# Layer 0's banded attention and the projection's first tiles, put in order by the kernel's list scheduler

## The chip, the cores and the metric

The kernel runs on one core of a Trainium2 chip. The core has a matrix engine (TensorE, PE in the profile; its weight loads are PEld), a vector engine (VectorE, DVE), a scalar engine (ScalarE, ACT), a general engine (GpSimd, POOL) and a queue engine that starts transfers (SyncE, SP). Each works through its own queue in order and waits on semaphores for the others. The metric is the device time of one execution in microseconds (us). TensorE's clock has two levels, 1.2 and 2.4 GHz; the profile gives it as a share of the upper one.

## The reference

Two transformer layers over 256 latent and 256 context tokens of width 1024, then a second block of another kind. All of it is fp32. Only layer 0's mixer matters here:

```
def even_mixer(u_ctx, u_lat, w_in, w_out, a_prm, sink, rope_ang, need_ctx):
    p_ctx = u_ctx @ w_in
    p_lat = u_lat @ w_in
    a_lat, a_ctx = rwkv7_mixer(p_ctx[..., :A_IN], p_lat[..., :A_IN], a_prm, need_ctx)
    qc, kc, vc = split_qkv(p_ctx[..., A_IN:], B_HEADS, B_KV_HEADS)
    ql, kl, vl = split_qkv(p_lat[..., A_IN:], B_HEADS, B_KV_HEADS)
    ql, kl = axial_rope(ql, rope_ang), axial_rope(kl, rope_ang)
    b_lat = banded_window_attention(ql, kl, vl, kc, vc, sink_g)
    b_ctx = context_attention(qc, kc, vc, sink_g)
    return concat(a_lat, b_lat) @ w_out, concat(a_ctx, b_ctx) @ w_out
```

One input projection feeds two things. Its attention part (8 query heads in two groups, 2 key and value heads, 64 wide) goes through a softmax that has a learned sink beside the scores. Its RWKV part is mixed with each token's neighbours (`centred_shift`) and then runs a recurrence in both directions. Layer 1 has two other kinds of attention; each layer ends with an MLP.

## The kernel before

**Products.** An fp32 operand is split into a high and a low part, and a product is three matmuls: high by high, high by low, low by high (`mmW`, lines 623 to 625). A weight chunk of 128x1024 comes by DMA into `raw`; ACT copies it to `whi` (line 608) and DVE subtracts to get `wlo` (line 609). In this part of the program the pool of `whi` and `wlo` has two buffers each.

**The stretch in question.** It has three pieces.

- Keys, values and four query tiles are projected over six PSUM tiles (`psT`). Each is evacuated by `evac_b`: an ACT copy into a ring of two buffers, rotary position (a matmul `psR`, line 944, and three DVE steps, lines 946 to 948) and the split into halves for the heads (`qB`, lines 962 and 963; `kBh` and `kBl`, lines 969 and 970).
- `b_attn` (line 1133) runs attention for 8 groups of four heads through `attn4`. For a head: scores in `psS` (two matmuls, line 1041, three PSUM banks in turn), the band's mask added by DVE (line 1048), the row maximum (line 1052), the sink (line 1057), the exponential on ACT with a sum (line 1059). For a pair of heads: the reciprocal and the normalisation of `P` on DVE and POOL (line 1068), the transposes `psP` (line 1077) and their copies to `PT`. Per group: eight output matmuls in `psO` (line 1087; one PSUM bank, written as halves of 64 columns of the array) and the split into `moBh` and `moBl` (lines 1090, 1091). The first four groups have 512 keys, the others 256.
- `proj_a` (lines 1134, 1135) computes 12 tiles of the RWKV part, each of 24 matmuls of 128x512 into `psT`, in two banks in turn. `evac_a` takes each out: an ACT copy with a scale (line 930) and two DVE steps for the neighbours (lines 931, 933). Tiles 12, 13 and 14 go to `lora`, the others to `rkv`.

Behind it the RWKV recurrence starts. Its first steps are kappa's square on DVE (`sq`), a sum over channels by matmul (`ssp`), a reciprocal root (`rsn`, on POOL) and its transposes (`psr`). Its pool (`rw`) lies where attention's buffers lay, so the square waits for the attention's last reader, a `psO` matmul.

**What sets the order.** There are two ways. Outside a marked stretch, the framework's own scheduler orders the instructions. Between `flow.open()` and `flow.close()` the kernel records every operation and orders it itself (class `_Flow`): `take` gives each operation an assumed duration, `links` its dependencies, including those by buffers in turn, and `order` issues, from what is ready first on the engine that can start first, the one with the longest chain behind it. For PE an operation of the current array shape has a bonus of 2000 ns. Neighbouring matmuls on the same tile are joined to one operation when short. The clock of this list starts at zero at the stretch's start: it does not know what the engines are still doing from before. Two stretches are ordered this way: the RWKV recurrence (`flow.open(2)`) and layer 1's attention (`flow.open()`). Everything issued so has the helper's line 501 in the profile. `b_attn` and `proj_a` were not in one.

Of the kernel before, what the change touches and what calls it, by code (L numbers as in the profile page):

```python
# [266 lines left out]
class _Flow:  # L267
# [47 lines left out]
    def take(self, key, op, f, a, k):  # L315
        is_ap = lambda x: isinstance(x, (tile.Tile, _View)) or isinstance(x, bass.AP) and isinstance(x.tensor, tile.Tile)
        aps = [x for x in list(a) + list(k.values()) if is_ap(x)]
        outs = [x for x in (a[0], k.get("accum_out")) if x is not None and is_ap(x)]
        o = _Op()
        o.key, o.calls, o.res = key, [(f, a, k)], [o]  # L320
        o.w = [self.touched(x) for x in outs]
        o.r = [self.touched(x) for x in aps if not any(x is y for y in outs)]
        n = math.prod(aps[0].shape[1:])
        psum = any(t_[3] for t_ in o.w + o.r)
        o.tail = 70
        if key == "T":
            mv, st = (a[1], a[1]) if op == "transpose" else (a[2], a[1])
            n = math.prod(mv.shape[1:]) if op != "transpose" else a[2].shape[1]
            size = lambda x: 32 if x <= 32 else 64 if x <= 64 else 128
            rows, cols = size(st.shape[0]), size(st.shape[1])  # L330
            cyc = 1 if mv.dtype == F32R else 2 if op == "transpose" else 4
            o.len, o.recs = max(n * cyc, 60 * min(cyc, 2)) / 2.4, 2 if cyc == 4 else 1
            o.cells = [(r, c) for r in range(4) if o.r[0][1] >> r & 1 for c in range(4) if o.w[0][1] >> c & 1]
            if mv.dtype == F32R:
                o.len += 11
            o.mode, o.tail, o.dur, o.grid, o.issue = (rows, cols), 270, 0, {}, 0
            o.first = op != "transpose" and k["start"] and not k.get("skip_group_check")
            o.more = op != "transpose" and not (k["start"] and k["stop"]) and not k.get("skip_group_check")
            o.parts = [(o.cells, o.len, o.recs)]
        elif key == "V":  # L340
            n = max(math.prod(x.shape[1:]) for x in aps)
            ins = sum(math.prod(x.shape[1:]) > 16 for x in aps if not any(x is y for y in outs))
            o.dur = 150 + 2.8 * n if op.endswith("scan") else 150 + 1.03 * n if psum else 170 + (self.both if ins > 1 else 1.2 if self.both > 1.5 else .65) * n
        elif key == "S":
            o.dur = 190 + .82 * n
        elif key == "G":
            o.dur = 1650 if k.get("op") == OP.pow else 200 + (1.3 if op == "tensor_scalar" and self.both > 1.5 else 2.4 if self.both > 1.5 or op != "tensor_scalar" else 3.2) * n
        elif key == "X":
            o.dur, o.tail = 0, 0
        else:  # L350
            o.dur, o.tail = 2800, 2500
        p = self.ops[-1] if self.ops else None
        if not (key == "T" and p is not None and p.key == "T" and p.mode == o.mode and
                (p.w[0][0] == o.w[0][0] and (p.dur < 800 or o.mode != (128, 128)) or self.one and p.one)):
            p = o
            self.ops.append(o)
        else:
            p.calls += o.calls
            p.res += o.res
            p.w += o.w  # L360
            p.r += o.r
            if key == "T":
                p.parts += o.parts
                p.first, p.more = p.first or o.first, p.more or o.more
        if key == "T":

            at = max([p.issue] + [p.grid.get(c, 0) for c in o.cells])
            p.issue = at + 7 * o.recs
            for c in o.cells:
                p.grid[c] = at + o.len  # L370
            p.dur = max(p.dur, p.issue, at + o.len)
            p.one = self.one
        return o
# [8 lines left out]
    def links(self):  # L382

        ops, seen = self.ops, {}
        for i, o in enumerate(ops):
            o.pre, o.at = set(), 0
            mine = [(x, True) for x in o.w] + [(x, False) for x in o.r]
            for (nm, q, m, ps), wr in mine:
                if isinstance(nm, _Root):
                    nm.ops.add(i)  # L390
                for j, q2, m2, wr2 in seen.get(nm, ()):
                    if q & q2 and ((wr or wr2) and m & m2 or ps and ops[j].key != o.key):
                        o.pre.add(j)
                    elif ps and q & q2 and wr and wr2 and o.key == "T" and o.first and ops[j].more and j != i:
                        o.pre.add(j)
            for (nm, q, m, ps), wr in mine:
                l = seen.setdefault(nm, [])
                if wr:
                    l[:] = [e for e in l if e[0] == i or e[1] & ~q or e[2] & ~m]
                l.append((i, q, m, wr))  # L400
        for g, names, ring in self.gates:
            k = ops.index(g)
            g.pre.update(i for i in range(k) if any(x[0] in names for x in ops[i].w + ops[i].r))
            for r in self.roots:
                if r.ring is ring:
                    for i in r.ops:
                        ops[i].pre.add(k)
        last = {}
        for r in self.roots:
            if r.heir is not None:  # L410
                was = {j for j, *_ in ()} | {i for i, o in enumerate(ops) if i < min(r.ops) and any(
                    x[0] is r.heir or x[0] == r.heir for x in o.w + o.r)}
            elif r.place is not None:
                was = last.get((id(r.ring), r.place), ())
                last[id(r.ring), r.place] = r.ops
            else:
                continue
            for i in r.ops:
                ops[i].pre.update(was)
        for i in range(len(ops) - 1, -1, -1):  # L420
            o = ops[i]
            o.way = getattr(o, "way", 0) + o.dur
            for j in o.pre:
                p = ops[j]
                p.way = max(getattr(p, "way", 0), o.way + (p.tail if p.key != o.key else 0))
# [81 lines left out]
def body(ctx: ExitStack, tc: tile.TileContext, A, out, dbg=None):  # L507
    nc = tc.nc
# [312 lines left out]
    def cpool(*cms):  # L821
        for cm in cms:
            opened.remove(cm)
            cm.__exit__(None, None, None)
# [305 lines left out]
    for t_ in S0s:  # L1130
        G.memset(t_, 0.0)

    b_attn()
    proj_a = lambda js, bank=None: gemm_T(W_in, [(j * 128, 128, j) for j in js], uh, ul, evac_a, bank=bank)
    proj_a((12, 13, 14) + tuple(x * 4 + t for t in range(3) for x in range(3)))
    cpool(cm_at, cm_attB)


# [1050 lines left out]
```

## Time and profile before

| | |
|---|---|
| median of 3 runs | 1804.53 us (1802.65 to 1807.39) |
| profiled execution | 1798.13 us, span 1796.2 us, mean clock 0.976 |
| PE busy | 1715.3 us (95%) |
| DVE, ACT, POOL busy | 60%, 49%, 25% |
| chain that ended last, PE | 86% |

The shares are means over the whole program. What one stretch can gain or lose is read from that stretch: whether PE waits in it, at which clock it runs, and which engine ends the waits. A wait appears in the timeline as a bracket behind the instruction that waited, with the engine and operation that released it.

### The profile page before, as it was taken

What the parts mean: (1) busy time and instruction counts of PE and PEld (TensorE: products, weight loads), DVE (VectorE), ACT (ScalarE), POOL (GpSimd) and SP (SyncE); (2) the same over time, 40 slices, a digit from 0 to 9 for tenths busy, and PEclk for the clock granted to TensorE, in tenths of its full rate; (3) what the DMA queues carried; (4) which work ended last, traced back from release to release, by engine and by line L of the source; (5) the groups of instructions that cost most, each with busy time, mean ns of one, the idle gap of its engine ahead of it and who ended that gap; (6) DMA issues with size and microseconds to landing.
All of it is one profiled execution on the core that took longest, in us unless ns stands there. A gap on an engine that the chain in (4) does not pass through costs nothing.

```text
span 1796.2 us, 33992 instructions
## 1 busy us (share of the span) xinstructions
PE 1715.3 (95%) x13601; PEld 1440.3 (80%) x13601; DVE 1082.0 (60%) x1965; ACT 884.1 (49%) x1703; POOL 447.2 (25%) x512
## 2 busy tenths in 40 slices
PE   6999899999898999999998999899989999999998
PEld 4777677767577888888887887799978889989997
DVE  3577577766656334444464775655566686568776
ACT  4555245544345554443443655545555554446553
POOL 1120344542413343333332213311120211110000
PEclk9999899999899999999998999999999999999999
DMA  9322141222264454444423322465547436655553
GB/s 311 108 59 60 37 140 51 96 74 95 72 198 142 131 169 147 141 141 141 141 82 87 89 71 71 132 197 187 188 152 226 129 93 174 190 156 187 177 183 121
DMA packets 185407, 240.08 MB, mean 134 GB/s; under 512 B 8961, under 2 KB 127889, under 8 KB 185121
## 3 DMA queue, kind: packets, MB, share of 16 engines
q1 hardware_dynamic: 183056, 229.68, 41.1%
q0 software_dynamic: 1904, 7.70, 1.3%
q8 instruction: 107, 1.75, 0.4%
q10 hardware_dynamic: 288, 0.52, 0.1%
q14 instruction: 52, 0.42, 0.1%
HBM read 236.83 MB, written 1.05 MB: 132 GB/s over the span
## 4 chain that ended last, share of the span: by engine, by line
PE 86%; DVE 5%; DMA 3%; ACT 2%; POOL 2%; issue 2%; SPq 0%; POOLq 0%; DVEq 0%; ACTq 0%
PE psT L623 9%; PE psT L625 9%; PE psT L624 9%; PE psT L501 9%; PE pf L628 6%; PE pf L629 6%; PE pf L630 6%; PE px L501 3%; PE ssp L501 2%; PE psr L501 2%; PE psU L623 2%; PE psU L625 2%; PE psU L624 2%; PE pq L501 2%; PE yp L501 2%; PE psS L501 2%
## 5 line engine op out<-in xcount | busy, mean ns | idle before, releaser
L609 DVE TENSOR_TENSOR wlo<-raw,whi 128x1024 fp32r<-128x1024 f32 x291 | 358.4, 1239 | 245.7 <-ACT whi L608 242.6
L608 ACT ACTIVATE whi<-raw 128x1024 fp32r<-128x1024 f32 x291 | 306.4, 1056 | 235.2 <-PE psT L624 121.6
L623 PE MATMUL psT<-uh,whi 128*128 128x256 f32 (+1 forms) x1032 | 332.4, 327 | 2.8 <-ACT uh L909 1.2
L624 PE MATMUL psT<-ul,whi 128*128 128x256 f32 (+1 forms) x1032 | 330.7, 321 | 0.0
L625 PE MATMUL psT<-uh,wlo 128*128 128x256 f32 (+1 forms) x1032 | 328.4, 321 | 0.0
L623 PEld LDWEIGHTS psT<-uh,whi 128*128 128x128 f32 x1032 | 193.3, 189 | 21.6 <-ACT uh L909 1.7
L624 PEld LDWEIGHTS psT<-ul,whi 128*128 128x128 f32 x1032 | 193.4, 188 | 17.9 <-issue 1.1
L625 PEld LDWEIGHTS psT<-uh,wlo 128*128 128x128 f32 x1032 | 193.5, 188 | 16.1 <-issue 0.3
L630 PE MATMUL pf<-whi,hlo 128*128 128x512 f32 x472 | 182.4, 390 | 0.0
L629 PE MATMUL pf<-wlo,hh 128*128 128x512 f32 x472 | 182.3, 390 | 0.0
L628 PE MATMUL pf<-whi,hh 128*128 128x512 f32 x472 | 181.9, 392 | 0.0
L1512 POOL TENSOR_TENSOR ffr<-ffr 128x512 f32<-128x512 f32 (+1 forms) x64 | 64.3, 1004 | 283.2 <-ACT hh L1511 251.7
L630 PEld LDWEIGHTS pf<-whi,hlo 128*128 128x128 f32 x472 | 88.6, 188 | 18.8 <-issue 0.2
L629 PEld LDWEIGHTS pf<-wlo,hh 128*128 128x128 f32 x472 | 88.6, 188 | 17.5
L628 PEld LDWEIGHTS pf<-whi,hh 128*128 128x128 f32 x472 | 88.5, 188 | 17.5
L623 PE MATMUL psU<-uh,whi 128*128 128x256 f32 x352 | 99.0, 282 | 1.0 <-DVE cv L2101 1.0
L624 PE MATMUL psU<-ul,whi 128*128 128x256 f32 x352 | 98.5, 280 | 0.0
L625 PE MATMUL psU<-uh,wlo 128*128 128x256 f32 x352 | 98.5, 280 | 0.0
L1513 DVE TENSOR_TENSOR hlo<-ffr,hh 128x512 fp32r<-128x512 f32 (+1 forms) x64 | 47.6, 743 | 76.9 <-POOL ffr L1512 76.9
L717 POOL TENSOR_TENSOR adac<-adac,wadc 128x512 f32<-128x512 f32 x56 | 76.2, 1361 | 64.0 <-ACT wadc L715 50.4
L715 ACT ACTIVATE wadc<-wadc,sT 128x512 f32<-128x512 f32 x56 | 40.5, 724 | 98.3 <-DMA wadc<-in_w_ada_dram 96.8
L623 PEld LDWEIGHTS psU<-uh,whi 128*128 128x128 f32 x352 | 66.6, 189 | 1.9 <-ACT whi L608 0.9
(775 smaller groups left out, 3603.1 us busy)
## 6 DMA issues: line engine op xcount, KB each, us to landing
raw<-in_w_ff_dram SPq DMA_DIRECT2D x128, 512.0 KB, 4.5
raw<-in_w_in_dram SPq DMA_DIRECT2D x50, 512.0 KB, 4.4
raw<-in_w_ada_dram SPq DMA_DIRECT2D x48, 512.0 KB, 4.7
raw<-in_w_ffn_up_dram SPq DMA_DIRECT2D x44, 512.0 KB, 4.8
wadc<-in_w_ada_dram SPq DMA_DIRECT2D x64, 256.0 KB, 2.9
raw<-in_w_out_dram SPq DMA_DIRECT2D x24, 512.0 KB, 3.7
raw<-in_w_ffn_down_dram SPq DMA_DIRECT2D x22, 512.0 KB, 4.5
raw<-in_w_in_even_dram SPq DMA_DIRECT2D x21, 512.0 KB, 4.2
```

What stands on the lines that cost most here:

```text
L501: b = f(*map(real, a), **{n: real(x) for n, x in k.items()})
L608: S.activation(hi[:, :tot], raw[:, :tot], AF.Copy)
L609: V.tensor_tensor(lo[:, :tot], raw[:, :tot], R(hi[:, :tot]), op=OP.subtract)
L623: T.matmul(p_, wh, xh, start=first, stop=False)
L624: T.matmul(p_, wh, xl, start=False, stop=False)
L625: T.matmul(p_, wl, xh, start=False, stop=last)
L628: T.matmul(p_, xh, wh, start=first, stop=False)
L629: T.matmul(p_, xh, wl, start=False, stop=False)
L630: T.matmul(p_, xl, wh, start=False, stop=last)
L717: G.tensor_tensor(acc, acc, w, op=OP.add)
L1512: G.tensor_tensor(r_, r_, r_, op=OP.mult)
L1513: V.tensor_tensor(hl_, r_, R(hh), op=OP.subtract)
```

## The change

`flow.open()` is put before `b_attn()` and `flow.close(...)` behind `proj_a(...)`, so both are recorded and issued in the list's order. The `rkv` tiles are then replaced by their real buffers. The links get a third flag (`head`) for a matmul that starts an accumulation with the group check off, as the 256-key scores do: another writer of the same PSUM bank has to wait for it. The assumed duration of a DMA falls from 2800 to 2000 ns except in the RWKV stretch, so that layer 1's list is drawn up with other numbers too.

```
+            o.head = op != "transpose" and k["start"] and not k["stop"] and k.get("skip_group_check")
...
-            o.dur, o.tail = 2800, 2500
+            o.dur, o.tail = 2800 if self.both > 1.5 else 2000, 2500
...
-                p.first, p.more = p.first or o.first, p.more or o.more
+                p.first, p.more, p.head = p.first or o.first, p.more or o.more, p.head or o.head
...
-                    elif ps and q & q2 and wr and wr2 and o.key == "T" and o.first and ops[j].more and j != i:
+                    elif ps and q & q2 and wr and wr2 and o.key == "T" and (o.first and ops[j].more or ops[j].head):
...
+    flow.open()
     b_attn()
     proj_a = lambda js, bank=None: gemm_T(W_in, [(j * 128, 128, j) for j in js], uh, ul, evac_a, bank=bank)
     proj_a((12, 13, 14) + tuple(x * 4 + t for t in range(3) for x in range(3)))
+    flow.close({x.engine for x in (nc.tensor, nc.vector, nc.scalar, nc.gpsimd)})
+    rkv.update({j: x.get() for j, x in rkv.items()})
```

The instructions are the same; their order on PE, DVE and ACT is not. Three places follow. Line numbers of the new program are one or more higher, and recorded operations carry line 502.

PE at the start of the stretch, before: scores (`psS`), the rotary matmul of the next query tile (`psR`) and projection matmuls (`psT`) alternate. The six `psT` here are the last of the query projection; the first of `proj_a` follow behind the last row.

```order
L1041 MATMUL psS<-kBh,qB 128x512
L1041 MATMUL psS<-kBl,qB 128x512
L944 MATMUL psR<-qB__685,cst_c_271 128x256
L623 MATMUL psT<-uh,whi 128x512
L624 MATMUL psT<-ul,whi 128x512
L625 MATMUL psT<-uh,wlo 128x512
L623 MATMUL psT<-uh,whi 128x512
L624 MATMUL psT<-ul,whi 128x512
L625 MATMUL psT<-uh,wlo 128x512
L1041 MATMUL psS<-kBh,qB 128x512
L1041 MATMUL psS<-kBl,qB 128x512
L944 MATMUL psR<-qB__703,cst_c_271 128x256
```

The same place now; above the first row stand the query projection's six `psT` and three more `psS`, and the last row is the first matmul of `proj_a`:

```order
L502 MATMUL psS<-kBl,qB 128x512
L945 MATMUL psR<-qB__703,cst_c_271 128x256
L502 MATMUL psS<-kBh,qB 128x512
L502 MATMUL psS<-kBl,qB 128x512
L945 MATMUL psR<-qB__721,cst_c_271 128x256
L502 MATMUL psS<-kBh,qB 128x512
L502 MATMUL psS<-kBl,qB 128x512
L502 MATMUL psS<-kBh,qB 128x512
L502 MATMUL psS<-kBl,qB 128x512
L502 MATMUL psS<-kBh,qB 128x512
L502 MATMUL psS<-kBl,qB 128x512
L502 MATMUL psT<-uh,whi 128x512
```

Six groups of two `psS` matmuls stand in front of the first projection matmul, where there were two; the first `psS` has moved behind the query projection's last six `psT`.

DVE at the end of a projection tile, before: the weight split of a later tile (`wlo`) and the two evacuation steps of one tile (`lora<-psT`), with attention's steps between them.

```order
L609 TENSOR_TENSOR wlo<-raw,whi 128x1024
L1082 COPY PT<-psP 128x512
L931 SCALAR_TENSOR_TENSOR lora<-psT,pv,lora 128x2x255
L1057 TENSOR_TENSOR nm<-nm,nsink 128x1
L1052 TENSOR_REDUCE nm<-psS 128x1
L1048 TENSOR_TENSOR psS<-psS,cst_cb 128x128
L933 SCALAR_TENSOR_TENSOR lora<-psT,pv,lora 128x2x255
```

Now, at the end of the second pair of tiles (14 into `lora`, 0 into `rkv_1009`):

```order
L502 TENSOR_TENSOR nm<-nm,nsink 128x1
L502 TENSOR_SCALAR P<-P,sums 128x512
L502 TENSOR_TENSOR wlo<-raw,whi 128x1024 x2
L502 SCALAR_TENSOR_TENSOR lora<-psT,pv,lora 128x2x255
L502 SCALAR_TENSOR_TENSOR rkv_1009<-psT,pv,rkv_1009 128x2x255
L502 SCALAR_TENSOR_TENSOR lora<-psT,pv,lora 128x2x255
L502 SCALAR_TENSOR_TENSOR rkv_1009<-psT,pv,rkv_1009 128x2x255
```

Two tiles now end together: two weight splits and four evacuation steps stand in one bunch. PE works on the two tiles of a pair in alternation, one in each of the two banks, each with one of the two weight buffers (in the first pair both tiles share a chunk of half the rows).

PE at the end of the stretch, before: the last `psO`, 23 more projection matmuls (`psT`), of which four stand here, and the first sum for kappa (`ssp`) behind the last of them.

```order
L1087 MATMUL psO<-PT,vBn 64x128 x4
L623 MATMUL psT<-uh,whi 128x512
L1087 MATMUL psO<-PT,vBn 64x128 x4
L624 MATMUL psT<-ul,whi 128x512
L625 MATMUL psT<-uh,wlo 128x512
L623 MATMUL psT<-uh,whi 128x512
L624 MATMUL psT<-ul,whi 128x512
```

Now:

```order
L502 MATMUL psT<-uh,wlo 128x512
L502 MATMUL psP<-cst_ci,P 128x128 x4
L502 MATMUL psO<-PT,vBn 64x128 x16
L502 MATMUL ssp<-cst_c_271,sq 128x2 x4
L502 MATMUL psr<-cst_ci,rsn 2x128 x4
```

The last transposes and the last sixteen `psO` stand behind the last projection matmul, right ahead of `ssp`.

## Rows read from the trace of the kernel before

**Rows 1.** The page's chain of work that ended last, shares by engine.

```profile
PE 86%; DVE 5%; DMA 3%; ACT 2%; POOL 2%; issue 2%; SPq 0%; POOLq 0%; DVEq 0%; ACTq 0%
```

**Rows 2.** By stretches: start:end and length, busy us (instructions) of each engine, PE's clock.

```profile
66.00:80.00 14.00, 10.60 (x39) 8.22 (x37) 9.97 (x20) 9.45 (x17) 0.58 (x4) 0.77 0.53 172
80.00:89.10 9.10, 9.10 (x40) 7.40 (x39) 8.85 (x23) 4.48 (x9) 0.00 (x0) 0.98 0.20 58
80.00:187.67 107.67, 107.67 (x641) 84.52 (x640) 78.57 (x200) 54.30 (x130) 14.67 (x8) 1.00 0.19 55
960.00:985.00 25.00, 21.04 (x128) 18.66 (x128) 6.00 (x8) 6.62 (x9) 4.60 (x4) 0.80 0.33 82
1000.00:1120.00 120.00, 119.85 (x817) 98.98 (x817) 78.78 (x154) 65.81 (x132) 31.79 (x28) 1.00 0.23 71
```

**Rows 3.** Timeline of PE, 70 to 89: start, us, line, operation, operands [idle before].

```profile
70.40 0.39 PE L625 MATMUL psT<-uh,wlo 128*128 128x512 f32 x1
74.19 0.79 PE L1041 MATMUL psS<-kBh,qB 128*128 128x512 f32 x1 [3.40 <-DVE qB L963]
...
79.97 0.79 PE L623 MATMUL psT<-uh,whi 128*128 128x512 f32 x1
...
88.70 0.39 PE L624 MATMUL psT<-ul,whi 128*128 128x512 f32 x1
88.93 0.39 PE L625 MATMUL psT<-uh,wlo 128*128 128x512 f32 x1
```

**Rows 4.** Timeline of DVE, 66 to 78.

```profile
66.47 1.22 DVE L609 TENSOR_TENSOR wlo<-raw,whi 128x1024 fp32r<-128x1024 f32 x1 [1.82 <-ACT whi L608]
...
73.45 1.41 DVE L963 TENSOR_TENSOR qB<-qB__667,qB 64x512 fp32r<-64x512 f32 x2
75.44 0.30 DVE L1048 TENSOR_TENSOR psS<-psS,cst_cb 128x128 f32<-128x128 f32 x1 [0.59 <-PE psS L1041]
75.78 0.69 DVE L1052 TENSOR_REDUCE nm<-psS 128x1 f32<-128x512 f32 x1
76.39 0.41 DVE L946 TENSOR_TENSOR ropeb<-psR,cst_c 128x256 f32<-128x256 f32 x1
...
77.05 0.15 DVE L1057 TENSOR_TENSOR nm<-nm,nsink 128x1 f32<-128x1 f32 x1
```

**Rows 5.** Timeline of ACT, 65 to 81.

```profile
77.36 0.69 ACT L1059 ACTIVATE P<-psS,nm 128x512 f32<-128x512 f32 x1 [1.82 <-DVE nm L1057]
77.95 0.19 ACT L1059 ACTIVATION_READ_ACCUMULATOR P<-psS,nm 128x1 f32 x1
...
79.33 1.06 ACT L608 ACTIVATE whi<-raw 128x1024 fp32r<-128x1024 f32 x1
```

**Rows 6.** Timeline of PE around a psO group; one psO matmul leaves two records.

```profile
122.12 0.39 PE L625 MATMUL psT<-uh,wlo 128*128 128x512 f32 x1
122.44 0.43 PE L1087 MATMUL psO<-PT,vBn 128*64 128x128 f32 x2
122.80 0.49 PE L623 MATMUL psT<-uh,whi 128*128 128x512 f32 x1
123.23 1.09 PE L1087 MATMUL psO<-PT,vBn 128*64 128x128 f32 x14
124.24 1.09 PE L1077 MATMUL psP<-cst_ci,P 128*128 128x128 f32 x8
```

**Rows 7.** Timeline of PE at the end of the stretch.

```profile
181.62 0.66 PE L1087 MATMUL psO<-PT,vBn 128*64 128x128 f32 x8
...
187.67 0.95 PE L501 MATMUL ssp<-cst_c,sq 128*128 128x2 f32 x8
191.32 0.60 PE L501 MATMUL psr<-cst_ci,rsn 128*2 128x128 f32 x4 [2.70 <-POOL rsn L501]
```

**Rows 8.** Timeline of DVE at the end of the stretch.

```profile
182.38 0.69 DVE L501 TENSOR_TENSOR sq<-kk 128x512 f32<-128x512 f32 x1 [5.24 <-PE psO L1087]
182.99 0.74 DVE L931 SCALAR_TENSOR_TENSOR rkv<-psT,pv,rkv 128x510 f32<-128x510 f32 x1
```

**Rows 9.** Timeline of PE at the start of layer 1's attention.

```profile
974.01 0.60 PE L501 MATMUL prk<-cst_ci,rky 128*2 128x128 f32 x4 [3.96 <-POOL rky L501]
```

## The prediction

> **What bounds the kernel now.** I read the chain that ended last first: TensorE (PE) carries 86% of it [rows 1], so what counts is whether PE's queue stands still, not how busy the others are. Then the table by stretches [rows 2]. The stretch that the change reorders is full: from 80.00 to 187.67 PE is busy in all 107.67 us at a granted clock of 1.00. Nothing can be gained there by filling gaps; only cheaper matmuls, or fewer switches between kinds of matmul, can shorten it. The stretch in front, 66 to 80, is the weak one: 10.60 of 14.00 us at a clock of 0.77. PE's timeline [rows 3] shows why: 3.40 us of waiting for VectorE's (DVE's) stacked queries, and after it the matmuls up to 79.97 at 1.2 GHz. As a pattern for the new order I took layer 1's attention, which the list scheduler already writes: 119.85 of 120.00 us busy between 1000 and 1120 [rows 2]. So the scheduler can fill a stretch; the question is whether it fills this one, with its own start and its own buffers.
>
> **The start.** Before, the first projection tile is spread between the first heads' scores. PE takes up projection matmuls at 79.97 [rows 3], and the forty records between 80.00 and 89.10 [rows 2] are 4 of psR, 4 of psS and 32 of psT. In the new order all six two-matmul groups of psS that the first six heads need stand in front of the first projection matmul. Six groups have three PSUM banks, so the fourth waits for the first head's exp, the fifth for the second's and the sixth for the third's. PE's queue is in order: the 32 projection matmuls stand behind them, although their weights could be split long before.
>
> When does the sixth group run? PE's last query matmul still ends at 70.79. The next now needs q1's evacuation on ScalarE (ACT), whose buffer is free only when DVE has stacked the keys, about 73.3 by the row of the next DVE step [rows 4]. One psR and six psT at the 0.43 us of 1.2 GHz bring the first psS to 76.7, against 74.19 before. From the first half of q1's stack (77.25) to the third head's maximum, DVE's queue now holds 26 instructions. By [rows 4] six half stacks (0.69, half of the row's 1.41), four reduces (0.69), six rope steps (0.41), four band adds (0.30) and six small ones (0.15) come to 11.5 us, and to about 9.8 when each starts some 0.07 before the one ahead of it has ended, as reduce, rope step and small step do in these rows. With some 0.5 of waiting for ACT's halves that is 87.6. The exp and its accumulator read take 0.88 [rows 5], so the sixth group starts near 88.5 and the first projection matmul near 89.1. Its weight split by ACT and DVE is ready at about the same time (0.5 us before), so PE's own order decides.
>
> At 89.1 the old order is 32 psT ahead, at 0.23 each [rows 3], 7.5 us, and the new one has two psS groups more, 0.9. Loss: 6.5 us. Nothing hides it, as PE never waits again until 187.67. Bounds: 4.5, if DVE and ACT overlap better than I walked them, and 8, if the half stacks wait for each other.
>
> **The clock after it.** After the 3.40 us wait PE ran 5.8 us at 1.2 GHz [rows 3]. In the new order PE stands still more than half of the time from 70.8 to 89.1. I expect it to enter the projection at 1.2 GHz and to need another 5.8 us to get out: 2.9 us lost. Bounds 0 (the clock rises during the psS groups) and 5.5 (as in the stretch 960 to 985, a clock of 0.80 after a wait of 3.96 us [rows 2, 9]). The Trainium skill, "TensorE: Matmul & The Clock Gate", section "What's actually happening", speaks against this part of the change: the throttled clock is the default there, and only activity lifts it. By that rule the 2.9 us is due, and the sum stays as it is; without it the sum would be 2.9 less. The trace agrees so far: 0.77 granted in the stretch with the wait.
>
> **The pairs of tiles.** Before, projection tiles run one after the other: while one is multiplied, the other bank and the other of two weight buffers are made ready. The new order runs two tiles in lockstep, both banks and both buffers at once, six pairs in all. So at the end of a pair both weight buffers and both banks come free together. From the second boundary on DVE does both splits and then four evacuation steps in alternation, so the first bank is ready after its third: with the first tile done 0.93 before the second, −0.93 + two ACT splits of 1.06 [rows 5] + one DVE split of 1.22 [rows 4] + three steps of 0.65 (0.74 each [rows 8], overlapping) = 4.4 us after the pair's last matmul. What PE has meanwhile is scores, transposes and outputs of the heads: about 4.1 and 3.7 us at the second and third boundary, 5.0 and 6.8 at the fourth and fifth, where reduces and normalisations push readiness to 6.0 and 7.8. Gaps: 0.3, 0.7, 1.0 and 1.0, none at the first, where the pair's first buffer comes free half-way. Sum 3.0 us. Bounds: 0, since layer 1's stretch in the same hand has 0.15 us of gaps in 120 [rows 2], though with four weight buffers, and 6.
>
> **The switches.** What speaks for the change: outputs psO (64 columns wide) stand in fewer and longer bunches, 8 instead of 22 by the two orders. In [rows 6] a psT, one psO, a psT and seven psO take 2.12 us from start to start; the two psT are 0.47, eight psO at 0.13 to 0.14 are 1.04 to 1.15; so 0.25 to 0.30 a bunch for getting in and out. Fourteen fewer: 3.5 to 4.2, I take 3.9. The upper bound is 7: matmuls alone are about 98.7 of the 107.67 us, so 9 are all that any switches cost, and some stay.
>
> **The end.** Before, 23 projection matmuls stand between the last psO (181.62) and the first ssp of the RWKV part, and cover DVE's square of kappa, which waits for the last psO because its buffer lies where the attention's lay (5.24 us of DVE idle [rows 8]). PE then waits 2.70 us, 3.65 from ssp to psr [rows 7]. In the new order the last 16 psO are PE's last work before ssp. That wait remains and the square comes uncovered in front of it: 0.17 + 0.69 + 0.06 = 0.9 us if DVE takes it at once, 1.7 behind one evacuation step [rows 8]. I take 1.4; bounds 0 and 3.
>
> **Smaller edits.** The assumed DMA time of 2.0 instead of 2.8 us also reorders a few matmuls in layer 1 and, as a consequence, where second normalisations fall; all still stand in full stretches: 0, bounds −1 and +1, but for the rival at 970 below. The flag in the links and the fetching of the projection's real buffers issue no instruction.
>
> **Sum.** 6.5 + 2.9 + 3.0 + 1.4 − 3.9 = 9.9 us. The profiled execution took 1798.13 (span 1796.2), so its like would take 1808.0. That execution lies 6.4 under the median of the runs shown, 1804.53; on the median I predict 1814.4, 0.55% slower.
>
> **Rivals.**
> 1. It packs as in layer 1 (other side). The start costs its lower bound of 4.5, the clock recovers while psS runs, the boundaries are covered, the end costs 0.9, and the switches bring 6: −0.6 us, 1803.9. For it: the 0.15 us in [rows 2] under the same scheduler. Against: six psS groups stand before the first projection matmul, which no packing later undoes. One quantity decides, PE's idle time between 70.8 and the first projection matmul: if that starts before 84, the forecast turns over, since 5 us of the sum go at once. It has ends on either side of no change, and a few us below.
> 2. Layer 1's start keeps its clock. One group of norm sums (pssk) moves five projection matmuls forward there, in front of the 3.96 us wait [rows 9]; that shortens the wait by about 0.6 and, if the clock then does not fall, saves the 5 us that the stretch from 974 to 985 loses: 9.9 − 5.6 = +4.3, 1808.8. Against: waits of 3.40 and 2.70 us let the clock fall as well [rows 3, 7].
> 3. The lockstep sets the pace. Readiness slips by a normalisation at each boundary, gaps are 6 in all, and PE drops once more to 1.2 GHz: +15.8, 1820.3. For it: both banks and both buffers come free at once; against: DVE has slack, 78.57 busy of 107.67 [rows 2]. The Trainium skill, "Perfetto Trace Analysis", section "Optimizing Tensor Performance", asks that independent groups of matmuls rotate through PSUM banks, so that the evacuation of one overlaps the next one's matmuls; the lockstep gives that up, and the trace of before, which keeps to it, shows no gap in 107.67 us.
>
> **How the numbers follow.** Forecast 0.55, rival 1 0.23, rival 2 0.08, rival 3 0.14. About 0.3%, 5.4 us, is what this kernel's measurement can tell from no change. Of the forecast 0.49 is slower and 0.06 within; rival 1 gives 0.10 faster, 0.12 within and 0.01 slower; rival 2 0.07 within, 0.01 slower; rival 3 is slower. Together 0.10 faster, 0.25 within, 0.65 slower. The forecast's own range is 1808 to 1820; to hold 8 in 10 over all cases it goes from 1801 to 1821.
>
> **What would show it.** Right: PE idle some 10 us in all between 70.8 and 89, first projection matmul near 89 at a clock of 0.5; waits of psT for ACT or DVE of about 1 us at the later pair boundaries; eight bunches of psO; kappa's ssp behind a wait of DVE. Wrong: a first projection matmul before 84, or a stretch from there to ssp shorter than the old 107.67 by more than 5 us, which would mean that switches cost more than I read from them.

## The result, and the profile after

The changed kernel takes 1819.13 us (median of 4 runs, 1816.55 to 1821.23); the kernel before, run beside it, 1803.59 (4 runs, 1800.10 to 1807.39). The ratio is 1.0077 [1.0057, 1.0098], which on 1803.59 is 13.9 us slower. Predicted were 1814.4 in a range of 1801 to 1821, and "slower" (by more than 0.3%) at 0.65. Run again in a later session it gave 1.0074 [1.0058, 1.0090], or 13.3 us. The profiled execution took 1817.81 (span 1816.0).

The chain of work that ended last in the changed kernel first; it answers to [rows 1]. PE's share fell from 86 to 83% and DVE's rose from 5 to 7%: PE now waits for others.

```profile
PE 83%; DVE 7%; ACT 3%; DMA 3%; issue 2%; POOL 2%; SPq 0%; POOLq 0%; DVEq 0%; ACTq 0%
```

The table by stretches of the changed kernel (columns as in [rows 2]):

```profile
80.00:90.90 10.90, 3.67 (x8) 1.92 (x9) 10.58 (x28) 7.44 (x15) 1.81 (x1) 0.74 0.00 0
90.90:196.30 105.40, 102.05 (x613) 82.10 (x611) 67.67 (x171) 47.66 (x118) 12.50 (x8) 0.98 0.22 61
196.30:208.00 11.70, 6.39 (x35) 3.17 (x33) 6.47 (x11) 0.77 (x2) 1.68 (x1) 0.71 0.06 15
```

The first row is the greater part of the loss: where PE was busy 9.10 of 9.10 us [rows 2], it is now busy 3.67 of 10.90, with 8 records instead of 40. DVE is nearly full there (10.58). The second row has 3.35 us of idle time where [rows 2] had none, and the third shows a ragged end.

What PE waited for between 60 and 240 us (us in total, times, longest):

```profile
PE psS L502 <- ACT P L502: 7.2, 5, 2.8
PE psR L945 <- ACT qB__685 L977: 2.7, 1, 2.7
PE psT L502 <- DVE rkv L502: 2.7, 3, 1.4
PE psO L502 <- DVE moBl L502: 2.1, 2, 1.5
PE psr L502 <- POOL rsn L502: 2.1, 1, 2.1
PE ssp L502 <- DVE sq L502: 1.7, 2, 1.0
```

The first line is the scores' waits for a PSUM bank, that is for the exp P that empties it. The longest wait of the third line and the whole fifth line lie behind the first ssp. PE's timeline at the start (answers to [rows 3]):

```profile
74.24 0.70 PE L945 MATMUL psR<-qB__685,cst_c 128*128 128x256 f32 x2 [2.69 <-ACT qB__685 L977]
...
82.51 0.50 PE L502 MATMUL psS<-kBh,qB 128*128 128x512 f32 x1 [1.01 <-ACT P L502]
...
85.88 0.79 PE L502 MATMUL psS<-kBh,qB 128*128 128x512 f32 x1 [2.64 <-ACT P L502]
...
89.88 0.80 PE L502 MATMUL psS<-kBh,qB 128*128 128x512 f32 x1 [2.79 <-ACT P L502]
90.47 0.63 PE L502 MATMUL psS<-kBl,qB 128*128 128x512 f32 x1
90.90 0.63 PE L502 MATMUL psT<-uh,whi 128*128 128x512 f32 x1
...
95.17 0.49 PE L502 MATMUL psT<-uh,whi 128*128 128x512 f32 x1
```

The fourth, fifth and sixth score group each stand still for an exp, and the projection's psT is queued behind them until 90.90. It then runs at 0.43 us a matmul until 95.17, and at 0.23 after that.

Two of the boundaries between pairs of tiles, where projection waits for an evacuation, in the same timeline:

```profile
121.52 0.50 PE L502 MATMUL psT<-uh,whi 128*128 128x512 f32 x1 [0.42 <-DVE lora L502]
...
155.06 0.50 PE L502 MATMUL psT<-uh,whi 128*128 128x512 f32 x1 [1.09 <-DVE rkv L502]
```

One bunch of outputs of the changed kernel (answers to [rows 6]), and PE's end of the stretch (answers to [rows 7]):

```profile
189.14 0.40 PE L502 MATMUL psT<-uh,whi 128*128 128x512 f32 x1
189.47 1.09 PE L502 MATMUL psO<-PT,vBn 128*64 128x128 f32 x16
190.50 0.50 PE L502 MATMUL psT<-ul,whi 128*128 128x512 f32 x1
190.84 0.39 PE L502 MATMUL psT<-uh,wlo 128*128 128x512 f32 x1
...
195.30 1.09 PE L502 MATMUL psO<-PT,vBn 128*64 128x128 f32 x16
197.86 1.09 PE L502 MATMUL psO<-PT,vBn 128*64 128x128 f32 x16 [1.47 <-DVE moBl L502]
199.91 1.02 PE L502 MATMUL ssp<-cst_c,sq 128*128 128x2 f32 x8 [0.95 <-DVE sq L502]
203.05 1.01 PE L502 MATMUL psr<-cst_ci,rsn 128*2 128x128 f32 x4 [2.11 <-POOL rsn L502]
```

From the first to the fourth row are 1.70 us; less two psT (0.47) eight psO cost 1.23, against 1.65 in [rows 6], where they stand in two bunches: 0.42 for one bunch fewer.

A measure for what follows is the **stretch**: from the first query tile's rotation to the first ssp, which is the same work in every kernel here. Before it goes from 68.81 to 187.67 [rows 7], 118.9 us; after, from 69.57 to 199.91, 130.3. So the stretch is 11.5 us longer, of 13.9 us in the median. Two traces with the old order there (before and e1) differ by 1.3 us in it, two of the changed kernel by 0.3: differences near 1 us are not read below. One trace stands behind each stretch.

### The profile page after: what moved, and what is told of

The parts are those of the page before. It is cut to its first block, busy times and chain, and to the rows that moved or that the text cites. A ratio compares the mean times of both kernels' runs of the same rounds, so it can differ in the third digit from the quotient of the medians.

```text
span 1816.0 us, 33968 instructions
## 1 busy us (share of the span) xinstructions
PE 1722.2 (95%) x13601; PEld 1446.0 (80%) x13601; DVE 1086.1 (60%) x1965; ACT 883.5 (49%) x1703; POOL 447.8 (25%) x512
## 4 chain that ended last, share of the span: by engine, by line
PE 83%; DVE 7%; ACT 3%; DMA 3%; issue 2%; POOL 2%; SPq 0%; POOLq 0%; DVEq 0%; ACTq 0%
PE psT L502 12%; PE psT L624 8%; PE psT L625 8%; PE psT L626 8%; PE pf L629 6%; PE pf L630 6%; PE pf L631 6%; PE px L502 3%; PE ssp L502 3%; PE psr L502 2%; PE pq L502 2%; PE psU L624 2%; PE psU L626 2%; PE psU L625 2%; PE psS L502 2%
## 5 line engine op out<-in xcount | busy, mean ns | idle before, releaser
L610 DVE TENSOR_TENSOR wlo<-raw,whi 128x1024 fp32r<-128x1024 f32 x279 | 344.9, 1244 | 234.7 <-ACT whi L609 230.5
L609 ACT ACTIVATE whi<-raw 128x1024 fp32r<-128x1024 f32 x279 | 293.5, 1056 | 222.9 <-PE psT L625 111.5
L624 PE MATMUL psT<-uh,whi 128*128 128x256 f32 (+2 forms) x936 | 293.8, 319 | 1.9 <-ACT uh L910 0.8
L625 PE MATMUL psT<-ul,whi 128*128 128x256 f32 (+2 forms) x936 | 292.9, 314 | 0.0
L626 PE MATMUL psT<-uh,wlo 128*128 128x256 f32 (+2 forms) x936 | 290.5, 314 | 0.0
L624 PEld LDWEIGHTS psT<-uh,whi 128*128 128x128 f32 (+1 forms) x936 | 175.4, 189 | 16.6 <-ACT uh L910 1.7
L625 PEld LDWEIGHTS psT<-ul,whi 128*128 128x128 f32 (+1 forms) x936 | 175.6, 188 | 14.2 <-issue 1.2
L626 PEld LDWEIGHTS psT<-uh,wlo 128*128 128x128 f32 (+1 forms) x936 | 175.6, 188 | 12.0 <-issue 0.2
L502 PE MATMUL psT<-uh,whi 128*128 128x512 f32 (+1 forms) x248 | 89.8, 374 | 3.4 <-DVE rkv L502 2.7
L502 PE MATMUL psT<-ul,whi 128*128 128x512 f32 (+1 forms) x248 | 89.1, 369 | 0.0
```

What stands on the lines that cost most here:

```text
L502: b = f(*map(real, a), **{n: real(x) for n, x in k.items()})
L609: S.activation(hi[:, :tot], raw[:, :tot], AF.Copy)
L610: V.tensor_tensor(lo[:, :tot], raw[:, :tot], R(hi[:, :tot]), op=OP.subtract)
L624: T.matmul(p_, wh, xh, start=first, stop=False)
L625: T.matmul(p_, wh, xl, start=False, stop=False)
L626: T.matmul(p_, wl, xh, start=False, stop=last)
```

## The experiments

The theory: the loss is made at the handover, since scores stand ahead of the projection in PE's queue; lockstep and end add to it. Rivals: the assumed DMA time, which also reorders layer 1; the lockstep as the chief cause; and the RWKV part behind the stretch, which also takes longer after the change. "Held" below is the edit of e3, "lift" that of e6, "lead" that of e4. Ratios are to the kernel before, run in the same session.

| run | us (median) | ratio | stretch, us |
|---|---|---|---|
| changed kernel | 1819.13 | 1.0077 [1.0057, 1.0098] | 130.3 |
| e5 changed again | 1816.66 | 1.0074 [1.0058, 1.0090] | 130.6 |
| e1 DMA time only | 1801.00 | 0.9989 [0.9973, 1.0005] | 117.6 |
| e2 five groups | 1809.89 | 1.0033 [1.0015, 1.0052] | 128.4 |
| e3 held | 1804.35 | 1.0003 [0.9987, 1.0020] | 122.6 |
| e4 lead | 1811.33 | 1.0039 [1.0019, 1.0059] | 128.3 |
| e6 lift | 1819.72 | 1.0092 [1.0065, 1.0119] | 137.9 |
| e7 held, lift | 1813.43 | 1.0061 [1.0043, 1.0079] | 132.2 |
| e8 held, lift, lead | 1808.28 | 1.0032 [1.0015, 1.0049] | 125.6 |
| e12 held, lead | 1808.47 | 1.0015 [1.0000, 1.0029] | 123.5 |
| e11 held, small lift, small lead | 1802.41 | 0.9986 [0.9974, 0.9999] | 119.8 |
| e9 two squares more | 1814.72 | 1.0051 [1.0036, 1.0065] | 132.1 |
| e10 four squares more | 1820.16 | 1.0086 [1.0071, 1.0102] | 133.5 |

The times do not follow the stretches one to one. By the ratios, e2 is 7.9 us faster than the changed kernel, e3 13.4 and e4 6.9, where their stretches are 1.9, 7.7 and 2.0 us shorter; e6 is 2.7 us slower with a stretch 7.6 longer. The rest lies outside the stretch ("What was unexpected" has a part of it). So the terms are read from the stretch, and an expected time that came out says little about its theory by itself.

What a stretch consists of can be worked out from its trace: the time in which PE is not busy (waits), what the lower clock costs (busy time by one minus the granted clock, in slices of 2 us), and the rest, which is the matmuls as they would take at the upper level. This is an estimate, since ends of matmuls are modelled.

| run | stretch, us | waits | lower clock | rest |
|---|---|---|---|---|
| before | 118.9 | 3.4 | 3.0 | 112.5 |
| e1 DMA time only | 117.6 | 3.4 | 1.6 | 112.6 |
| changed kernel | 130.3 | 15.8 | 4.9 | 109.6 |
| e2 five groups | 128.4 | 15.2 | 2.9 | 110.3 |
| e3 held | 122.6 | 10.8 | 1.6 | 110.2 |
| e4 lead | 128.3 | 14.7 | 4.8 | 108.8 |
| e12 held, lead | 123.5 | 10.6 | 4.9 | 108.0 |
| e11 held, small lift, small lead | 119.8 | 8.6 | 3.3 | 107.9 |

**e1: the DMA time alone,** in the kernel before.

```diff
-            o.dur, o.tail = 2800, 2500
+            o.dur, o.tail = 2800 if self.both > 1.5 else 2000, 2500
```

> The old program with only the assumed DMA time of the list lowered from 2.8 to 2.0 us; attention and projection of layer 0 stay with the framework's scheduler. Theory A (the loss lies in layer 0's stretch: the scores put ahead of the projection, the pairs of tiles, the end): as the kernel before, within 2 us, and the first ssp of the RWKV part at 187 to 188. Theory B (a part of the loss comes from layer 1's new list and from what follows it): 3 to 6 us slower than before, with the added time behind 960 us.

No change that can be measured, a stretch of 117.6 and the first ssp at 187.00. Through layer 1's list this part of the change is not the cause. In the changed kernel the same number also shapes layer 0's new list, as e2 shows.

**e2: fewer score groups ahead of the projection,** by the list's assumed DMA time in the changed kernel.

```diff
-            o.dur, o.tail = 2800 if self.both > 1.5 else 2000, 2500
+            o.dur, o.tail = 2800 if self.both > 1.5 else 1700, 2500
```

> The changed kernel with an assumed DMA time of 1.7 instead of 2.0 us outside the RWKV stretch: in layer 0's list one of the six groups of scores moves behind the first projection pair, the rest of the stretch stays as it is. Theory A: the first projection matmul no longer waits for the third head's exp and starts at 86 to 87.5 instead of 90.9, the first ssp comes 3 to 4 us earlier (196 to 197 instead of 199.9), the time is 3 to 4 us below the changed kernel. Theory C (the start only moves a wait that comes back later, since heads and tiles are short of VectorE and of buffers all the same): the first projection matmul earlier, but ssp at 199 to 200 and the time within 1 us of the changed kernel.

The stretch fell by 1.9, less than expected. Counted from the rotation (70.88 in e2, 69.57 after), the fifth and last group starts 4.0 us earlier than the changed kernel's sixth, but the next in line is late; PE's timeline of e2:

```profile
87.18 0.79 PE L502 MATMUL psS<-kBh,qB 128*128 128x512 f32 x1 [2.33 <-ACT P L502]
...
91.19 0.79 PE L502 MATMUL psT<-uh,wlo 128*128 128x512 f32 x1 [1.75 <-DVE wlo L502]
```

The weight's low half is now awaited, because DVE's queue has the heads' steps ahead of that split. One group fewer on PE uncovers the same backlog on DVE: the waits of the stretch are 15.2 us, against 15.8, and what it gained is clock. Its ssp, at 199.29, came where theory C had it; its time fell by more than either theory said.

**e3, "held": the list is told that the weights' transfers began 8 us earlier.**

```diff
+        if o.key == "Q":
+            return -8000
...
-    flow.open()
+    flow.open(held=(0, 0, 0, 0))
```

> The changed kernel with one addition to the list: weight transfers count as begun 8 us before the stretch, so the list has the first projection weights at once. Three groups of scores stand ahead of the first projection matmul instead of six; the pairs of tiles, the bunches of outputs and the end stay much as they are. Theory A: projection runs from about 81 instead of 90.9 and the clock is up by 86, ssp comes 8 to 10 us earlier, at 190 to 192, and the time is 8 to 10 us below the changed kernel, 4 to 6 above the one before. Theory C: ssp at 198 to 200, the time within 2 us of the changed kernel.

This gives back 7.7 of the 11.5 us of the stretch, just short of what was expected. The ratio falls to 1, which is more than the 8 to 10 us expected, and more than the stretch explains. The table by stretches of e3, to set beside the first row of after:

```profile
80.00:91.00 11.00, 10.17 (x43) 8.01 (x44) 10.33 (x25) 5.48 (x13) 0.69 (x1) 1.00 0.33 95
```

PE is busy 10.17 of 11.00 us at a clock of 1.00. Its timeline has the projection running from 79.27:

```profile
79.27 0.39 PE L512 MATMUL psT<-uh,whi 128*128 128x512 f32 x1
```

A part of the gain comes back later, as theory C had it for all of it: two score groups wait 1.45 and 0.85 us for P, where the changed kernel waits 0.39 twice.

**e4, "lead": one tile of a pair is preferred,** so that the two finish apart.

```diff
+            o.pri = self.lead if o.key == "T" and any(turn.get(x[0], 1) % 2 == 0 for x in o.w if isinstance(x[0], _Root)) else 0
...
-                key=lambda i: (ops[i].way + (stay if ...
+                key=lambda i: (ops[i].way + ops[i].pri + (stay if ...
...
-    flow.open()
+    flow.open(lead=12000)
```

The preference is 12000 ns.

> The changed kernel with a preference in the list for one tile of each pair, so that tiles run one after the other and not in lockstep; the start with six groups of scores stays, five tiles then stand ahead of the transposes, and the last outputs still stand right ahead of ssp. Theory A: first projection matmul at 90 to 91 as in the changed kernel; the 2 us of waits of psT for the evacuation go, the end costs as much or 1 us more: time 0 to 3 us below the changed kernel. Theory D (the lockstep is the main loss): 6 us or more below the changed kernel.

2.0 us of the stretch come back, and only 1.1 of them are waits, against 3.4 of waits that I put down to the pairs below. The time is 6.9 us below the changed kernel, which was the sign set for theory D. It does not decide for D, since the RWKV part is 5.9 us shorter in e4's trace (275.9 against 281.8 us from the first px matmul to the last, see e9). One boundary is still late in e4's timeline:

```profile
154.00 0.50 PE L505 MATMUL psT<-uh,whi 128*128 128x512 f32 x1 [1.50 <-DVE rkv L505]
```

**e5: the changed kernel again,** without an edit.

> The changed kernel itself, run beside the others, since one program's executions differ by up to 17 us with the clock that TensorE is granted in the RWKV part. Theory A (what counts is layer 0's stretch, 11.5 us longer from the first query tile's rotation to the first ssp in the trace): the stretch again 130 to 131 us, the median 10 to 13 us over the kernel before. Theory E (the change also makes the RWKV part slower, 282 instead of 276 us from its first to its last state update in the two traces): 15 to 19 us over, and that part at 281 or more again.

It repeats: a stretch of 130.6, and all six runs between 1816.03 and 1817.75. By the ratio it is 13.3 us over the kernel before, just above theory A's 10 to 13 and below E's 15 to 19, while the RWKV part took 281.9 us, as E had it. The stretch alone is not the whole loss.

**e6, "lift": the last two outputs are made urgent,** so that projection is left to cover the end.

```diff
+        outs = [r for r in self.roots if r.name == "psO"][-2:]
...
+            o.lift = self.lift if any(x[0] is r for x in o.w for r in outs) else 0
-            o.way = getattr(o, "way", 0) + o.dur
+            o.way = getattr(o, "way", 0) + o.dur + (o.lift if o.key == "T" else 0)
...
-    flow.open()
+    flow.open(lift=4000)
```

> The changed kernel with the last two groups' outputs counted as 4 us more urgent in the list, which stands for kappa's square, of which the list knows nothing: eight projection matmuls stand behind the last psO, and the outputs come in more and shorter bunches. The start is unchanged. Theory A: the waits of 1.5 and 1.0 us around the last psO go, at 0.3 us for each further bunch: the first ssp 1 to 2 us earlier and psr 2 us earlier, the time 0 to 3 us below the changed kernel. Theory F (the end is a main loss, as PE starts the RWKV part at 1.2 GHz because of it): 4 us or more below.

The opposite happened: the stretch grew by 7.6, though the waits around the last psO are gone. The time rose less, by 2.7, with runs from 1812.77 to 1827.80. PE's timeline of e6 shows why the stretch grew:

```profile
175.06 0.47 PE L504 MATMUL psT<-uh,whi 128*128 128x512 f32 x1 [2.33 <-DVE rkv L504]
...
192.12 0.77 PE L504 MATMUL psT<-uh,whi 128*128 128x512 f32 x1 [3.26 <-DVE rkv L504]
...
207.84 1.17 PE L504 MATMUL ssp<-cst_c,sq 128*128 128x2 f32 x8 [2.21 <-DVE rkv L504]
```

With the heads done early, the last pairs of tiles have little beside them, and the boundaries of these pairs cost 2.2 to 3.3 us. In the changed kernel, where the heads' work stands beside them, they cost at most 1.1.

**e7: held and lift.** The two edits together.

```diff
...
-    flow.open()
+    flow.open(held=(0, 0, 0, 0), lift=4000)
```

> Both additions to the list at once: the first weights count as landed, and the last outputs are more urgent; tiles still go in lockstep. Theory A, where the terms add: the stretch from the first query tile's rotation to ssp 120 to 123 us, since the start's gain (7.8) stands and the end gains 1 to 2: the time 2 us under to 2 us over the kernel before. Theory C (gains at the start come back as waits of the heads): stretch 125 or more.

Missed, by the mechanism of e6: 132.2, on theory C's side of 125. In e7's timeline:

```profile
184.09 0.76 PE L517 MATMUL psT<-uh,whi 128*128 128x512 f32 x1 [3.27 <-DVE rkv L517]
```

**e8: held, lift and lead.**

```diff
...
-    flow.open()
+    flow.open(held=(0, 0, 0, 0), lift=4000, lead=12000)
```

> All three additions: weights landed, one tile at a time, last outputs more urgent. Theory A, where the terms add (start 7.8, lockstep 2.0, end 1 to 2 of the 11.5 us): the stretch is 118 to 121 us, as long as before within 2 us, and the time 3 us under to 2 us over the kernel before. If fewer bunches are worth the 3 us that the sum gives them, and no wait takes their place, 117 or less and 2 to 4 us under.

Missed as well: 125.6, and 5.8 us over the kernel before. With one tile far ahead of the other three long waits stand in the stretch. PE's timeline of e8:

```profile
95.76 0.60 PE L517 MATMUL psT<-uh,whi 128*128 128x512 f32 x1 [2.41 <-ACT whi L517]
...
125.10 0.50 PE L517 MATMUL psT<-uh,whi 128*128 128x512 f32 x1 [2.43 <-DVE lora L517]
...
187.04 0.47 PE L517 MATMUL psT<-uh,whi 128*128 128x512 f32 x1 [3.01 <-DVE es L517]
```

One is for a split on ACT, the others are boundary waits for an evacuation on DVE, so those have not gone. The last names es, a step of the heads that projection does not read; DVE's step right in front of es is an evacuation into rkv, which ends at 186.89.

**e9 and e10: the RWKV part moved in time.** The changed kernel, with kappa's first square computed three and five times over, so that ssp comes later and nothing else is altered.

```diff
...
+                        for _ in range(self.again):
+                            f(*map(real, a), **{n: real(x) for n, x in k.items()})
...
-    flow.open(2)
+    flow.open(2, again=2)
```

In e10 `again` is 4.

> The changed kernel with kappa's first square computed three times over instead of once on VectorE, right in front of the first ssp: the RWKV part starts 1.2 us later, in the same order and with the same waits. Theory E (the changed kernel's RWKV part is a fixed 282 us, from its new neighbours): the part again 281 to 283 us, the median 1 to 2 us over the changed kernel's 1816.7. Theory G (that part's length depends on when its pauses fall, as TensorE's clock falls for shorter or longer after each of them, and the old program shows both 276 and 282): the part leaves 282 us in the trace or in most executions, so that the median drops by 2 us or more although work is added, or the executions spread over 8 us and more instead of 2.

> The same with the square computed five times: the RWKV part starts 2.5 us later than in the changed kernel. Theory E: the part 281 to 283 us, the median 2 to 4 us over the changed kernel. Theory G: another length of the part than 282 us, or executions that spread over 8 us and more, and a median that does not follow the added 2.5 us.

The two disagree. ssp's wait for the square grew from 0.95 to 2.62 us in e9 and to 4.07 in e10. By the ratios e9 is 9.2 us over the kernel before, which is 4.1 less than e5, and e10 15.5, which is 2.2 more. What the RWKV part itself took shows in the row of its 880 px matmuls (first and last start), which is the same program in all kernels. Before, e1 and after, in this order:

```profile
L501 PE MATMUL px<-Sp,Qm x880: 216/218/366, 228.1 to 503.7; 64*64 64x64 f32 x176
```

```profile
L501 PE MATMUL px<-Sp,Qm x880: 216/218/366, 227.1 to 509.2; 64*64 64x64 f32 x176
```

```profile
L502 PE MATMUL px<-Sp,Qm x880: 216/218/366, 240.2 to 522.0; 64*64 64x64 f32 x176
```

That is 275.6, 282.1 and 281.8 us; in e9 it is 279.0, in e10 281.3. So the old order can take 282 as well, and in e4, e7, e8 and e11, which all have the new one, it is 275.2 to 275.9. Whether a shift in time sets it is not decided by two runs that point different ways.

**e12: held and lead.**

```diff
...
-    flow.open()
+    flow.open(held=(0, 0, 0, 0), lead=12000)
```

> The list with the first weights landed and one tile at a time; the end as in the changed kernel, outputs last. Theory A, where the start (7.8 us) and the lockstep (2.0 us) add: stretch 120 to 121.5 us, time 0 to 3 us under the kernel before. Theory C (a gain at the start comes back as waits of the heads, which run later): 123 us or more.

Missed: 123.5, no better than e3's 122.6, and 2.7 us over the kernel before. Its waits are as long as e3's in all (10.6 and 10.8 us). Two are long in e12's timeline, one of them at a boundary:

```profile
96.05 0.50 PE L517 MATMUL psT<-uh,whi 128*128 128x512 f32 x1 [3.39 <-ACT whi L517]
...
120.57 0.47 PE L517 MATMUL psT<-uh,whi 128*128 128x512 f32 x1 [1.68 <-DVE rkv L517]
```

The first costs more than its length. From 96.05 to 102.00 the clock granted is 0.55, and over the stretch the lower clock costs 4.9 us, where e3 loses 1.6.

**e11: held, with a small lift and a small lead.**

```diff
...
-    flow.open()
+    flow.open(held=(0, 0, 0, 0), lift=1500, lead=3000)
```

> The list with the first weights landed, a small preference for one tile of a pair (3 us) and a small urgency of the last outputs (1.5 us): bunches of 16 outputs up to the last three, eight projection matmuls before the last transposes, eight outputs right ahead of ssp. Theory A: start as in the run with landed weights, no waits of psT at pair boundaries, the end at 1 to 2.5 us of waits: stretch from the first query tile's rotation to ssp 119 to 122 us, time 0 to 3 us under the kernel before. Theory C: 123 us or more, and no gain over the run with landed weights alone.

Theory A's numbers came out: a stretch of 119.8, and 0.9986 [0.9974, 0.9999], or 2.5 us under the kernel before. It is the one version of the new order whose ratio lies below 1; e3's interval includes 1 as well. The waits at pair boundaries that were to go have not all gone (1.79). PE's timeline of e11:

```profile
94.50 0.47 PE L517 MATMUL psT<-uh,whi 128*128 128x512 f32 x1 [1.79 <-DVE lora L517]
...
129.85 0.50 PE L517 MATMUL psS<-kBh,qB 128*128 128x512 f32 x1 [1.97 <-ACT P L517]
```

Its stretch is no shorter than before's 118.9, so nothing here shows that the reordering itself wins time: by the table above its matmuls take 4.6 us less, and its waits 5.2 more. Where the small gain in the median is from stays open.

## Why the prediction was right, step by step

| term | predicted | measured after |
|---|---|---|
| start | 6.5 | 7.5 |
| clock after it | 2.9 | 2.0 |
| pairs of tiles | 3.0 | 3.4 |
| end | 1.4 | 2.4 |
| switches | -3.9 | -3.8, by remainder |
| sum, the stretch | 9.9 | 11.5 |

- **The start** held in mechanism and place. First projection matmul at 90.90 instead of 89.1; PE's five waits in front of it sum to 10.0 us, as the text said. Measured from the rotation, 90.90 is 21.33 us in, when the old order was 36 projection matmuls ahead (8.4 us) and two score groups behind (0.93): 7.5. Counted as waits alone (10.0 against 3.4) it is 6.6. That it is the chief loss is shown by e3, where the same list with one assumption altered starts the projection at 79.27 and wins 7.7 us back, clock included. The exps came later than I walked them: DVE is busy 10.58 of the 10.90 us from 80.
- **The clock** fell as predicted, but its price was luck in part. Ten matmuls between 90.90 and 95.17 at 0.43 instead of 0.23 are 2.0 us. I had carried over the whole 5.8 us at the lower clock of [rows 3]; but only 5.3 were left after the last wait, and 1.0 of those went to the sixth score group. How long PE stays at the lower level behind a wait is not fixed in these traces: 5.8 us behind the 3.40 of before, 3.8 behind the 2.69 at 74.24 after, and in e2 behind the same 2.69 the clock granted is 1.00 from 70.88 to 78.00. e3, without the waits, has a clock of 1.00 where the changed kernel has 0.74. The Trainium skill ("TensorE: Matmul & The Clock Gate", "What's actually happening") calls the throttled clock the default that activity lifts. The traces agree: 0.74 where PE was busy 3.67 of 10.90 us, 1.00 in e3 where it was busy 10.17 of 11.00.
- **The pairs** held in sum, partly by luck. psT waits 0.18, 0.42, 0.20 and 1.09 us at the first four boundaries, 1.9 in all, where I had none, 0.3, 0.7 and 1.0. Scores and outputs between 135 and 178 us wait another 1.5 (psS 0.39 twice, psO 0.68), which I had not counted; my fifth gap of 1.0 is not there as a psT wait. e4, which was to take these waits away, has 1.1 us of waits less in all. The price of a boundary with little beside it, 2.2 to 3.3 us, I had not worked out; e6 and e7 show it.
- **The end** had the right wait and missed another. kappa's square makes ssp wait 0.95 us, as predicted. But the last outputs have one PSUM bank, so the second bunch also waits 1.47 us for the first one's copy out (moBl), which DVE does behind rkv steps. DVE's timeline of the changed kernel (answers to [rows 8]):

```profile
195.47 0.75 DVE L502 SCALAR_TENSOR_TENSOR rkv<-psT,pv,rkv 128x510 f32<-128x510 f32 x1 [2.83 <-ACT rkv L502]
196.14 0.68 DVE L502 COPY PT<-psP 128x512 f32<-128x512 f32 x1
196.74 0.74 DVE L502 SCALAR_TENSOR_TENSOR rkv<-psT,pv,rkv 128x510 f32<-128x510 f32 x1
197.39 0.42 DVE L502 TENSOR_TENSOR moBl<-psO,moBh 128x256 fp32r<-128x256 f32 x1
197.72 1.40 DVE L502 SCALAR_TENSOR_TENSOR rkv<-psT,pv,rkv 128x510 f32<-128x510 f32 x2
199.07 0.69 DVE L502 TENSOR_TENSOR sq<-kk 128x512 f32<-128x512 f32 x1
```

- **The switches** stand in the table as what remains of the sum. The second table of the experiments gives them without a remainder: the rest is 112.5 and 112.6 us in both traces of the old order and 109.6 after, 2.9 less, and with the start at 6.6 the terms again make 11.5. That is 0.2 us for each of the 14 bunches, where I took 0.28. The bunch above saves 0.42; 14 of those would be 5.9, and the stretch does not show so much. No run changes the bunches alone.
- **Smaller edits** at nothing: e1 agrees for the DMA time; the flag in the links was not run by itself. Rival 2, a shorter wait at layer 1's start, is there as a wait (3.2 instead of 3.96 us [rows 9]), but the clock falls all the same, to 0.80 from 985 to 1010 as from 960 to 985 before [rows 2]. e1 has the shorter wait too (3.1), and no gain that can be measured. The fall behind the 2.70 us of [rows 7], which I named against this rival, does not show in those rows; the trace of before grants 0.57 from 192 to 200.
- **Rival 1** fell with its own sign: the projection starts at 90.90, not before 84. What it described comes nearest to e11.
- **Rival 3** had the mechanism that e6 and e7 show, but not the changed kernel, whose boundaries wait at most 1.1 us.
- **What the sum lacked** is the 2.4 us between the stretch's 11.5 and the ratio's 13.9. The RWKV part's px rows take 6.2 us more in after's profiled execution than in before's, with nearly the same list of waits and a clock of 0.93 against 0.96. The forecast had no term for this part: of the 4.0 us between its 9.9 and the measured 13.9, 1.6 are sizes of its terms and 2.4 lie here. Since e1 has 282.1 with the old order, this length is not made by the change alone; that all ten runs of the changed kernel lie between 1816 and 1821.3 while the kernel before spreads from 1793 to 1813 suggests that it falls into the long form nearly always. Why stays open.

## What to carry to other kernels

A list scheduler that starts its clock at zero for every stretch does not know what each engine has still to do, nor what has already landed: look at the first thing it puts into the in-order queue of the bounding engine, and ask when its inputs are really there. Two tiles in lockstep free their buffers together, so the boundary needs other work beside it as long as it is (here up to 3.3 us). A priority that spends this other work early can cost more than it gives, as the 7.6 us of e6. Terms that are each recoverable alone need not add up: in e7, e8 and e12 a wait came in another place or on another engine, and in e12 the clock fell behind it.

## What was unexpected

The RWKV part, in one order and with nearly the same waits, took 275.2 to 282.1 us in the 14 traces of this study. Its length goes with the granted clock: 0.95 or 0.96 in the five traces of up to 275.9 us, 0.93 or 0.94 in the six of 281.3 or more, with e3, e9 and e12 between. PE's busy time in it is 257.7 us before and 263.7 after, so PE does not wait longer: it works slower. In these two traces the clock falls at the same three places, each behind waits of PE, and it is lower after the change (before and after): 0.91 and 0.83 over the 20 us from 80 us behind the first px, 0.91 and 0.74 over the 20 from 150, 0.79 and 0.74 over the 40 from 230. Why it stays low for longer is open. The 6.9 us between the ends are half of the loss that was to be explained, and about as much as the largest single term. So a reordering that ends at 200 us is measured through a part that it does not touch.
